# A 4096-cubed matmul with bias and tanh: the start reordered, with the first eight k-tiles in two blocks of four

One core of one Trainium2 chip. The metric is device time in microseconds (us) of one execution; the median of several runs is quoted.

## The reference

```python
def reference(a, b, bias):          # all float32, 4096 x 4096, bias 4096
    return np.tanh(np.matmul(a, b) + bias)
```

The kernel works in fp16: loads cast fp32 to fp16 on the way, issued from GpSimd.

## The kernel before

The matmul needs A with k on the partitions, so A must be turned. Column chunk 0 (1024 columns, two PSUM banks wide) is special: its start has nothing loaded yet, so row blocks 0 to 3 ("group 0", eight PSUM banks) go over k-tiles 0 to 7 first, then row blocks 4 to 7 ("group 1") over the same k-tiles, then both over k-tiles 8 to 15, and so on; partial sums are put aside in SBUF. I call each of the first passes of 64 matmuls a block of 64.

```python
KS = 8          # the k order of the first 8 k-tiles: k = 8*x + t, x = partition
def load_b_low(queue, dst, n0, t0, nt):           # B: every 8th row is one k-tile
    src = b[ds(0, P * KS), ds(n0, NCW)].rearrange("(x t) n -> x t n", t=KS)
    queue.dma_start(out=dst, in_=src[:, ds(t0, nt), :])
...
def load_nat(m):                                  # row-wise A, 4 KB runs, 8 k-tiles
    nc.gpsimd.dma_start(out=nat[m], in_=a[ds(m * P, P), ds(0, P * KS)]...)
def turn_nat(m):                                  # 8 TensorE transposes, 2 copies
    ...
# order of the queue: A0 A1 B1 A2 B2 A3 B3 B4 B5 B6 B7, then
want_a("g1a", 2, 4 * P, 2 * Q, 0, KS)             # row blocks 4,5: 4 loads of 128 KB
want_a("g1b", 2, 6 * P, 2 * Q, 0, KS)             # row blocks 6,7: 4 loads of 128 KB
want_a(("g0", KS), G, 0, G * Q, KS, KM - KS)      # group 0, k-tiles 8..15
... B k-tiles 8..15, group 1 k-tiles 8..15, A and B k-tiles 16..31, bias ...
for m in range(G):
    turn1(m, ("g1a", "g1b"), 0, KS)               # VectorE transposes
down(ps, KS - 2, KS, put_aside)                   # k-tiles 6,7 of group 0
group1(0, KS, put_aside, before1)                 # second block of 64
```

`load_a` issues one DMA for each quarter of 32 partitions and each stretch of k order, so for row blocks 8 to 31 and all later chunks 4 loads for k-tiles 0 to 7 and 4 for 8 to 31.

## Time and profile before

| | kernel before |
|---|---|
| median (3 runs; a fourth came with the result) | 1785.42 us (1785.22 to 1785.9) |
| profiled span | 1783.5 us |
| TensorE busy | 1776.8 us |
| second block of 64 starts | 25.25 us |
| third block starts | 39.08 us |
| sixth pass (row blocks 4 to 7, k-tiles 16 to 31) starts | 94.33 us |
| the remaining 7712 matmuls start | 121.96 us |

From 121.96 us on the kernel is one unbroken run of matmuls. The lines are in the prediction.

### The profile page before, as it was taken

Reading aid. Unit: us, or ns where it says so; the run is one execution under the profiler, and the core shown is the slowest. Engines: PE = TensorE matmul, PEld = TensorE weight load, DVE = VectorE, ACT = ScalarE, POOL = GpSimd, SP = SyncE. Lnnn points to the kernel's source line nnn. Section 1 sums busy time; section 2 is a strip of 40 time slices with the busy share of each in tenths; the row PEclk is TensorE's granted clock in tenths of the full one; section 3 lists DMA queues with packets and bytes.
Section 4 is the critical chain, followed back from the end, with each engine's and each line's share of the span. In section 5 each row is a group of like instructions: output and inputs, shape, how many; then the busy total and the mean of one; then the engine's idle time right before and its main releaser. Section 6 shows DMA issues by size and latency. Waiting matters only on the chain.

```text
span 1783.5 us, 20275 instructions
## 1 busy us (share of the span) xinstructions
PE 1776.8 (100%) x8272; PEld 808.7 (45%) x8272; DVE 856.6 (48%) x561; ACT 174.9 (10%) x281; POOL 607.3 (34%) x1126
## 2 busy tenths in 40 slices
PE   9999999999999999999999999999999999999999
PEld 4444444444444444444444444444444444444444
DVE  3774544455444544454444544454445544454442
ACT  3020000000000000000000000000000000000001
POOL 5454433232443333223343333223322233223310
PEclk9999999999999999999999999999999999999999
DMA  9999987676988866666698876666767666766731
GB/s 194 189 211 222 172 151 129 111 136 110 191 155 154 149 107 119 116 119 118 111 201 154 158 135 118 113 121 107 130 111 125 107 111 118 118 114 108 119 75 42
DMA packets 207916, 238.61 MB, mean 134 GB/s; under 512 B 22096, under 2 KB 157776, under 8 KB 207824
## 3 DMA queue, kind: packets, MB, share of 16 engines
q0 software_dynamic: 170384, 169.68, 65.2%
q1 hardware_dynamic: 37152, 67.52, 10.4%
q8 instruction: 64, 1.05, 0.2%
q14 instruction: 28, 0.23, 0.0%
q10 hardware_dynamic: 288, 0.13, 0.0%
HBM read 337.64 MB, written 67.11 MB: 227 GB/s over the span
## 4 chain that ended last, share of the span: by engine, by line
PE 99%; DMA 0%; issue 0%; POOL 0%; ACT 0%; DVE 0%; POOLq 0%; DVEq 0%
PE ps L404 93%; PE ps L134 6%; DMA nat<-in_a_dram 0%; POOL nat L231 0%; PE tp L243 0%; ACT o_sb L148 0%; DVE at L245 0%; DVE o_sb L145 0%; ACT at L246 0%; POOL b L68 0%; POOL ident L251 0%; POOLq L251 0%; DVEq L145 0%; POOLq L427 0%
## 5 line engine op out<-in xcount | busy, mean ns | idle before, releaser
L404 PE MATMUL ps<-b,at 128*128 128x512 f16 x7712 | 1657.8, 378 | 0.0
L404 PEld LDWEIGHTS <-at 128*128 128x128 f16 x7712 | 754.6, 98 | 903.3
L85 POOL DMA_DIRECT2D an<-in_a_dram x1004 | 542.4, 549 | 1059.4 <-DVE at L96 921.8
L96 DVE STREAM_TRANSPOSE at<-an 128x1024 f16<-128x1024 f16 x252 | 647.7, 2612 | 0.1
L145 DVE TENSOR_TENSOR o_sb<-ps,bias_bc 128x512 f32<-128x512 f32 (+1 forms) x243 | 166.2, 685 | 873.6 <-PE ps L404 752.4
L148 ACT ACTIVATE o_sb<-o_sb 128x512 f32<-128x512 f32 (+1 forms) x243 | 151.7, 625 | 1500.9 <-DVE o_sb L145 1500.9
L134 PE MATMUL ps<-b,at 128*128 128x512 f16 x256 | 56.4, 379 | 1.4 <-DVE at L245 1.0
L72 POOL DMA_DIRECT2D b<-in_b_dram x96 | 52.2, 548 | 14.3 <-DMA an<-in_a_dram 10.3
L134 PE MATMUL ps<-b,atx 128*128 128x512 f16 x256 | 55.8, 379 | 0.0
L134 PEld LDWEIGHTS <-at 128*128 128x128 f16 x256 | 24.8, 98 | 31.5 <-DVE at L245 1.9
L134 PEld LDWEIGHTS <-atx 128*128 128x128 f16 x256 | 24.9, 98 | 30.3 <-DVE atx L96 0.3
L96 DVE STREAM_TRANSPOSE atx<-an 128x1024 f16<-128x1024 f16 (+1 forms) x12 | 21.9, 1897 | 16.6 <-DMA an<-in_a_dram 16.6
L148 ACT ACTIVATE spill<-spill 128x512 f32<-128x512 f32 x16 | 9.9, 630 | 78.5 <-DVE spill L145 78.5
L68 POOL DMA_DIRECT2D b<-in_b_dram x13 | 8.3, 643 | 24.7 <-PE ps L404 22.6
L145 DVE TENSOR_TENSOR spill<-ps,spill 128x512 f32<-128x512 f32 x16 | 10.3, 675 | 9.0 <-PE ps L134 9.0
L176 DVE TENSOR_TENSOR spill<-spill,bias_bc 128x512 f32<-128x512 f32 x16 | 9.7, 683 | 7.3 <-DMA bias_bc<-in_bias_dram 7.3
L171 DVE TENSOR_TENSOR spill<-ps,spill 128x512 f32<-128x512 f32 x16 | 10.2, 676 | 4.3 <-PE ps L134 4.3
L168 ACT COPY spill<-ps 128x512 f32<-128x512 f32 x16 | 8.7, 605 | 15.7 <-PE ps L134 15.7
L245 DVE COPY at<-tp 128x512 f16<-128x512 f16 x4 | 1.7, 425 | 11.8 <-PE tp L243 11.8
L219 PE MATMUL ps<-zeros 128*128 128x512 f16 x16 | 5.5, 522 | 1.3 <-DVE zeros L215 1.3
L219 PEld LDWEIGHTS <-zeros 128*128 128x128 f16 x16 | 2.0, 128 | 4.3 <-issue 2.5
L243 PE MATMUL tp<-ident,nat 128*128 128x128 f16 x32 | 2.7, 228 | 0.4 <-DMA nat<-in_a_dram 0.3
(13 smaller groups left out, 12.9 us busy)
## 6 DMA issues: line engine op xcount, KB each, us to landing
an<-in_a_dram POOLq DMA_DIRECT2D x480, 192.0 KB, 6.5
out_dram<-o_sb SPq DMA_DIRECT2D x239, 256.0 KB, 3.4
an<-in_a_dram POOLq DMA_DIRECT2D x480, 64.0 KB, 2.5
b<-in_b_dram POOLq DMA_DIRECT2D x103, 256.0 KB, 8.5
b<-in_b_dram POOLq DMA_DIRECT2D x6, 1024.0 KB, 13.6
an<-in_a_dram POOLq DMA_DIRECT2D x32, 128.0 KB, 6.5
out_dram<-spill SPq DMA_DIRECT2D x16, 256.0 KB, 5.7
an<-in_a_dram POOLq DMA_DIRECT2D x12, 256.0 KB, 7.2
```

What stands on the lines that cost most here:

```text
L68: queue.dma_start(out=dst, in_=src[:, ds(t0, nt), :])
L72: nc.gpsimd.dma_start(out=bt[t0 // TB][ds(q * QP, QP), ds(t0 % TB, nt), :], in_=src.rearrange("(t p) n -> p t n", p=QP),)
L85: nc.gpsimd.dma_start(out=an[ds(q * QP, QP), :, ds((t - t0) * QP, n * QP)], in_=src.rearrange("(mb p) k -> p mb k", p=QP),)
L96: nc.vector.transpose(at[:, ds(t, n), :].rearrange("P t (mb p) -> P mb t p", p=QP), an[:, ds(mb0, Q), ds((t - t0) * QP, n * QP)].rearrange ...
L134: nc.tensor.matmul(ps, at[:, t, :], bt[t // TB][:, t % TB, ts(j, NB)], start=start, stop=stop)
L145: nc.vector.tensor_tensor(out=o_sb[:, piece], in0=ps[:, piece], in1=addend[:, piece], op=mybir.AluOpType.add)
L148: nc.scalar.activation(o_sb[:, piece], o_sb[:, piece], mybir.ActivationFunctionType.Tanh)
L168: nc.scalar.copy(aside(m, j), ps)
L171: nc.vector.tensor_tensor(out=aside(m, j), in0=ps, in1=aside(m, j), op=mybir.AluOpType.add)
L176: nc.vector.tensor_tensor(out=aside(m, j), in0=aside(m, j), in1=bias_bc[:, ts(j, NB)], op=mybir.AluOpType.add)
L219: nc.tensor.matmul(warm, zeros[:, :P], zeros, start=i == 0, stop=i == WARM - 1)
L404: nc.tensor.matmul(ps, at[:, t, :], b_cur[t // TB][:, t % TB, ds(c0, w)], start=t == 0, stop=t == KT - 1,)
```

## The change

The intent: start TensorE sooner. Cut the k order of the first eight k-tiles into two blocks of four. Then row-wise A needs only 128 KB (written) per row block for the first four k-tiles, and all four can go ahead of B's second tile. The second block of group 0 comes later, for VectorE; row block 4 is loaded row-wise and turned by TensorE in the middle of the pass. The core of the diff:

```diff
+    BL = 4
-    WARM = 16
+    WARM = 12
-        src = b[ds(0, P * KS), ds(n0, NCW)].rearrange("(x t) n -> x t n", t=KS)
+        src = b[ds(t0 // BL * BL * P, P * BL), ds(n0, NCW)].rearrange("(x t) n -> x t n", t=BL)
+    def split(t0, nt):           # load_a and transpose_a: 4 + 4 + rest, was 8 + rest
+        low = [(t, BL) for t in range(t0, min(t0 + nt, KS), BL)]
+        t = max(t0, KS)
+        return low + ([(t, t0 + nt - t)] if t0 + nt > t else [])
-    load_nat(0)
-    load_nat(1)
-    ... B1, A2, B2, A3, B3 .. B7
-    want_a("g1a", 2, 4 * P, 2 * Q, 0, KS)
-    want_a("g1b", 2, 6 * P, 2 * Q, 0, KS)
+    for m in range(G):
+        load_nat(m, 1)                       # A0 A1 A2 A3, k-tiles 0..3
+    for i in range(3):
+        want(load_b_next)                    # B1 B2 B3
+    want_a("g0a", 2, 0, 2 * Q, BL, BL)       # group 0, k-tiles 4..7: 8 loads of 64 KB
+    want_a("g0b", 2, 2 * P, 2 * Q, BL, BL)
+    for i in range(3):
+        want(load_b_next)                    # B4 B5 B6
+    want(lambda: load_nat(G, KS // BL))      # row block 4
+    want(load_b_next)                        # B7
+    want_a("g1a", 2, 5 * P, 2 * Q, 0, KS)    # row blocks 5,6: 8 loads of 64 KB
+    want_a("g1b", 1, 7 * P, Q, 0, KS)        # row block 7: 8 loads of 32 KB
... (loops of the first pass rewritten to match; row block 4 turned inside down())
```

More of the change, by code (lines that the diff above doesn't have):

```diff
@@ L65, in load_b_low @@
     def load_b_low(queue, dst, n0, t0, nt):
-        src = b[ds(0, P * KS), ds(n0, NCW)].rearrange("(x t) n -> x t n", t=KS)
-        queue.dma_start(out=dst, in_=src[:, ds(t0, nt), :])
+        src = b[ds(t0 // BL * BL * P, P * BL), ds(n0, NCW)].rearrange("(x t) n -> x t n", t=BL)
+        queue.dma_start(out=dst, in_=src[:, ds(t0 % BL, nt), :])
     def load_b(bt, n0, t0, nt, q):
@@ L75, in load_b @@
         )
+    def split(t0, nt):
+        low = [(t, BL) for t in range(t0, min(t0 + nt, KS), BL)]
+        t = max(t0, KS)
+        return low + ([(t, t0 + nt - t)] if t0 + nt > t else [])
     def load_a(m0, nmb, t0, nt):
         an = anat.tile([P, nmb, nt * QP], fp16, name="an")
-        parts = [(0, KS), (KS, t0 + nt - KS)] if t0 < KS < t0 + nt else [(t0, nt)]
-        for t, n in parts:
+        for t, n in split(t0, nt):
             for q in (0, 2, 1, 3):
-                k = q * KS * QP if t < KS else P * KS + (q * (KT - KS) + t - KS) * QP
+                k = t * P + q * BL * QP if t < KS else P * KS + (q * (KT - KS) + t - KS) * QP
                 src = a[ds(m0, nmb * QP), ds(k, n * QP)]
@@ L91, in transpose_a @@
     def transpose_a(at, an, mb0, t0, nt):
-        parts = [(0, KS), (KS, t0 + nt - KS)] if t0 < KS < t0 + nt else [(t0, nt)]
-        for t, n in parts:
+        for t, n in split(t0, nt):
             order = "P mb (k t) -> P mb t k" if t < KS else "P mb (t k) -> P mb t k"
@@ L194, in across, with down @@
                     mm(ps[m][j], ats[m], b_cur, t, j, t == first, False)
-    def down(ps, t0, t1, done):
+    def down(ps, t0, t1, done, before=None):
         for m in range(G):
+            if before:
+                before(m)
             for j in range(J):
@@ L225, with load_nat @@
     nc.scalar.copy(b_cur[0][:, 0, :], raw_b[:, 0, :])
-    nat = [opool.tile([P, P, KS], fp16, name=f"nat_{m}", tag="o_sb") for m in range(G)]
-    def load_nat(m):
+    def load_nat(m, blocks):
+        nat = opool.tile([P, blocks, P, BL], fp16, name="nat", tag="o_sb")
+        src = a[ds(m * P, P), ds(0, blocks * P * BL)]
         nc.gpsimd.dma_start(
-            out=nat[m], in_=a[ds(m * P, P), ds(0, P * KS)].rearrange("m (x t) -> m x t", t=KS)
+            out=nat, in_=src.rearrange("m (u x t) -> m u x t", u=blocks, t=BL)
         )
+        nats[m] = nat
     def load_b_next():
@@ L238, in load_b_next, with turn_nat @@
         load_b_low(nc.gpsimd, b_cur[t // TB][:, ds(t % TB, 1), :], 0, t, 1)
-    def turn_nat(m):
-        tp = psum.tile([P, KS, P], fp16, name="tp", tag="ps")
-        for t in range(KS):
-            nc.tensor.transpose(tp[:, t, :], nat[m][:, :, t], ident)
-        h = KS // 2
-        nc.vector.tensor_copy(ats[m][:, ds(0, h), :], tp[:, ds(0, h), :])
-        nc.scalar.copy(ats[m][:, ds(h, h), :], tp[:, ds(h, h), :])
-    b_done = [1]
-    load_nat(0)
-    load_nat(1)
+    def turn_nat(m, blocks, copy):
+        tp = psum.tile([P, blocks * BL, P], fp16, name="tp", tag="ps")
+        for t in range(blocks * BL):
+            nc.tensor.transpose(tp[:, t, :], nats[m][:, t // BL, :, t % BL], ident)
+        copy(ats[m][:, ds(0, blocks * BL), :], tp)
+    nats, b_done = {}, [1]
+    for m in range(G):
+        load_nat(m, 1)
     nc.gpsimd.affine_select(
@@ L254, with row @@
     )
-    load_b_next()
-    for m in (2, 3):
-        load_nat(m)
-        load_b_next()
-    while b_done[0] < KS:
-        load_b_next()
-    want_a("g1a", 2, 4 * P, 2 * Q, 0, KS)
-    want_a("g1b", 2, 6 * P, 2 * Q, 0, KS)
+    for i in range(3):
[4 more added lines that the diff above has]
+        want(load_b_next)
+    pump()
+    ps = []
+    def row(m, t0, nt):
+        if len(ps) == m:
+            ps.append([psum.tile([P, NB], fp32, name="ps") for j in range(J)])
+        across(ps, (m,), t0, nt, 0)
+    turn_nat(0, 1, nc.vector.tensor_copy)
+    turn_nat(1, 1, nc.scalar.copy)
+    row(0, 0, 1)
+    turn_nat(2, 1, nc.vector.tensor_copy)
+    row(1, 0, 1)
+    turn_nat(3, 1, nc.scalar.copy)
+    row(2, 0, 1)
+    row(3, 0, 1)
+    across(ps, range(G), 1, BL - 1, 0)
+    want(lambda: load_nat(G, KS // BL))
+    want(load_b_next)
+    want_a("g1a", 2, 5 * P, 2 * Q, 0, KS)
+    want_a("g1b", 1, 7 * P, Q, 0, KS)
     want_a(("g0", KS), G, 0, G * Q, KS, KM - KS)
@@ L277, with before0 @@
     todo = [(c, mi) for c in range(NC) for mi in range(MT) if (c, mi) >= (0, 2 * G)]
-    ps = []
-    def row(m, t0, nt):
-        if len(ps) == m:
-            ps.append([psum.tile([P, NB], fp32, name="ps") for j in range(J)])
-        across(ps, (m,), t0, nt, 0)
-    turn_nat(0)
-    turn_nat(1)
-    row(0, 0, 1)
-    row(1, 0, 1)
-    across(ps, (0, 1), 1, 1, 0)
-    turn_nat(2)
-    row(2, 0, 2)
-    across(ps, (0, 1, 2), 2, 1, 0)
-    turn_nat(3)
-    row(3, 0, 3)
-    across(ps, range(G), 3, KS - 2 - 3, 0)
-    def turn1(m, keys, t, nt):
-        turn(ats[G + m], keys[m // 2], (m % 2) * Q, t, nt)
+    for m in range(G):
+        turn(ats[m], "g0a" if m < 2 else "g0b", m % 2 * Q, BL, BL)
+    across(ps, range(G), BL, KS - 2 - BL, 0)
+    def before0(m):
+        if m == 2:
+            turn_nat(G, KS // BL, nc.vector.tensor_copy)
+    down(ps, KS - 2, KS, put_aside, before0)
     def turn0(m, t, nt):
         turn(ats[m], ("g0", t), m * Q, t, nt)
-    for m in range(G):
-        turn1(m, ("g1a", "g1b"), 0, KS)
-    down(ps, KS - 2, KS, put_aside)
     def before1(m, j):
         if m == G and j == 0:
+            turn(ats[5], "g1a", 0, 0, KS)
+            turn(ats[6], "g1a", Q, 0, KS)
+            turn(ats[7], "g1b", 0, 0, KS)
             for i in range(G):
@@ L318 @@
     for m in range(G):
-        turn1(m, ("g1c", "g1d"), KS, KM - KS)
+        turn(ats[G + m], "g1c" if m < 2 else "g1d", m % 2 * Q, KS, KM - KS)
     across(ps, range(G), KS, KM - 2 - KS, KS)
```

## The prediction

> **What bounds the kernel now.** I first read the busy rows of the page and the chain that ended last, then its start in order of time.
>
> ```profile
> span 1783.5 us, 20275 instructions
> PE 1776.8 (100%) x8272; PEld 808.7 (45%) x8272; DVE 856.6 (48%) x561; ACT 174.9 (10%) x281; POOL 607.3 (34%) x1126
> ```
>
> TensorE is busy over the whole span. The work is 32 k-tiles x 32 row blocks x 8 column banks = 8192 matmuls of 512 columns. The chain shows how little else there is:
>
> ```profile
> 8.07 2.15 PE L134 MATMUL ps<-b,at 128*128 128x512 f16 x8
> ...
> 11.58 2.33 PE L134 MATMUL ps<-b,at 128*128 128x512 f16 x10 [0.52 <-DVE at L245]
> ...
> 14.93 0.39 PE L134 MATMUL ps<-b,at 128*128 128x512 f16 x1 [0.52 <-DVE at L245]
> 15.54 9.87 PE L134 MATMUL ps<-b,at 128*128 128x512 f16 x45 [0.22 <-ACT at L246]
> 25.25 13.99 PE L134 MATMUL ps<-b,atx 128*128 128x512 f16 x64
> 39.08 13.98 PE L134 MATMUL ps<-b,at 128*128 128x512 f16 x64
> ```
>
> These are TensorE's lines in order of time (start, length, what). From 15.54 us to the end there is no gap. A block of 64 matmuls takes 39.08 - 25.25 = 13.83 us, 0.216 us each (the 379 ns that the page gives as the mean of one is a latency). So only two things can move the time: when the gapless run begins, counted by how many matmuls were done before it, and whether the change opens a new gap later. I use one marker: the start of the second block of 64 (row blocks 4 to 7 on k-tiles 0 to 7), 25.25 us now. Whatever moves it moves the end.
>
> Before 15.54 us 19 matmuls are done (4.1 us of work), so 11.4 us of the span are lost there. After 8.07 us the loss is 25.25 - 8.07 - 64 x 0.216 = 3.4 us, mostly the 16 late transposes of A and waits for their copies. The idle that the change attacks is thus at most about 5 us: 1.5 us of earlier first matmul and 3.4 us, against 1785.
>
> What feeds that start? The transfers:
>
> ```profile
> nat<-in_a_dram POOLq DMA_DIRECT2D x4, 256.0 KB, 6.2
> ```
>
> ```profile
> DMA packets 918, 1.66 MB, mean 207 GB/s; under 512 B 101, under 2 KB 110, under 8 KB 918
> ```
>
> ```profile
> DMA packets 3159, 1.55 MB, mean 194 GB/s; under 512 B 132, under 2 KB 3159, under 8 KB 3159
> ```
>
> The second fence is the DMA view from 10 to 18 us (2 KB packets), the third from 20.5 to 28.5 us (512 B packets). Both windows are full, at about 200 GB/s of written fp16. In the records the 256 KB loads land every 1.25 us (12.77, 14.03, 15.31, 16.52, 17.78, 19.09 us), so the start is a saturated queue. B's last low tile (k-tile 7, eleventh in the queue) lands at 19.09 us:
>
> ```profile
> L68 POOL DMA_DIRECT2D b<-in_b_dram x1: 531/531/531, 9.0 to 9.0; - x1
> ...
> DMA to landing us min/median/max: 10.1/10.1/10.1
> ```
>
> TensorE wants it only at 25.25 - 16 x 0.216 = 21.8 us: 2.7 us of slack. That slack is what the change can spend.
>
> **What the Trainium skill says.** "DMA: Bandwidth & Descriptors", section "Why small descriptors are slow (HBM only)", gives each packet a fixed overhead of a few cycles; its "Specifications" want at least 512 B for line rate. The trace agrees mildly down to 512 B: from 2048 to 512 B the rate drops from 207 to 194 GB/s. It has no 256 B load, which is what the change makes. "TensorE: Matmul & The Clock Gate", section "Part 1: The HAM clock gate", says about 3.4 us of work warm the array and that an idle window as long cools it. In the trace the warm-up matmuls go from 0.43 us apart to 0.215 at 5.08 us, 3.8 us after the first. Twelve of them end at about 5.5 us, so cutting 16 to 12 is safe, provided that no wait comes near 3.4 us.
>
> **The change part by part.**
>
> *Earlier first matmul.* Row-wise A loads halve (128 KB written each) and all four go ahead of B's tile 1. They take the queue places that two old ones had: half-sized steps on the old landings (5.88, 7.48, 8.73, 10.30) put them at about 5.3, 5.9, 6.7 and 7.5 us. Four transposes each (8 took 0.71 us), a copy of 0.42 us on VectorE or 0.59 on ScalarE: first matmul at about 6.6 us instead of 8.07, k-tile 0 finished at about 9.2. B tiles 1 to 3 are queue places 3 to 5 and land at about 8.75, 10.3 and 11.55, so TensorE runs without a gap to about 14.4 us with 32 matmuls done, where the old kernel had 19 at 15.54.
>
> *Then the queue is the bound.* Before B's tile 7, the old queue held 4 x 256 of A plus 7 x 256 KB of B: 2816 KB. The new one holds 512 KB of row-wise A, 512 KB of A's second block (8 loads of 64 KB in 256 B packets), 256 KB of row block 4 and 1792 KB of B: 3072 KB, 256 KB more, hence 1.25 us. Packets: from 1.25 us for sixteen 2048 B packets per engine and 0.67 us for sixteen of 512 B, one packet costs about 4 ns + 0.0746 ns/B; 256 B then take 23 ns, 176 GB/s, 0.38 us per 64 KB (estimate, a straight line beyond its points). Eight of them cost 3.0 instead of 2.5 us, and the 1 KB packets another 0.1 us. B's tile 7 then lands at 19.09 + 1.25 + 0.5 + 0.1 = 21.0 us. The same arithmetic puts B's tile 4 at 15.9 us: TensorE waits 14.4 to 16.0 there, and again about 1.6 us for tile 7, because at 19.4 us it has done everything else. Behind tile 7 lie 16 matmuls (3.45 us) and the 8 transposes of row block 4 (about 0.8): the second block of 64 begins at about 21.1 + 4.3 = 25.4 us. That is **0.15 us later** than now. The 256 KB more ahead of tile 7 eat the slack, so the better beginning buys nothing.
>
> *What comes after.* A's load for row blocks 5 to 7 is now 16 loads, in 64 and 32 KB pieces. GpSimd needs 0.55 to 0.58 us to issue each, more than the 0.2 us that a 32 KB piece moves for; also an issue waits until the load eight before it has landed (the issue at 9.02 us follows the landing at 8.73). I put A and B for k-tile 8 about 3 us later than now, B's at 39 to 40 us against 35.96. TensorE wants it at 39.2, so a stall of 0 to 0.8 us is possible there: I add **0.2 us**. Transposes for row blocks 5 to 7 must be ready from about 28.9 us on, with data about 25 us and 2.1 us of VectorE for a block:
>
> ```profile
> L96 DVE STREAM_TRANSPOSE atx<-an 128x1024 f16<-128x1024 f16 x4 | 8.0, 2170 | 8.1 <-DMA an<-in_a_dram 8.1
> ```
>
> They are in time.
>
> *The other 1700 us.* The order view shows that each later row block now has 12 loads of A instead of 8 (120 row blocks, 480 more issues) and three VectorE transposes instead of two. GpSimd: 14 issues with B's two x 0.55 = 7.7 us in the 13.8 us of a row block. DMA: 512 packets of 512 B become 1024 of 256 B, 16 x (2 x 23 - 41) = 80 ns per 64 KB on an engine, 0.16 us a row block. VectorE: one fixed cost of some 0.1 us. TensorE is fed two row blocks ahead, so all of it lies beside the matmuls: **0**.
>
> *Sum.* 0.15 + 0.2 = 0.35 us; the uncertainty of 256 B packets is one-sided (150 GB/s instead of 176 adds about 0.5 us on tile 7's landing, 100 GB/s adds 2.2), so I put the centre at +0.6: 1785.42 + 0.6 = **1786.0 us**.
>
> **Rivals.**
> 1. *The whole early gain survives.* If tile 7 did not bind, the second block would begin at 6.6 + 64 x 0.216 + 2 = about 22.4 us: 1782.6. For it: TensorE's idle at 10 to 15 us does go away. Against it: the queue is full from 5 us on at 207 GB/s, and 3072 KB cannot be through by 18 us. A quicker queue start by half a us would give 1785.
> 2. *256 B packets are slow* (100 GB/s or less). Then A's second block takes 5.2 us, tile 7 lands at 23.2, the second block starts at 27.6, and k-tile 8 comes late too: 1788 to 1789. For it: the page's 512 B rule. Against: the small loss from 2048 to 512 B.
> 3. *Steady state opens gaps.* Were the later row blocks bound by DMA or by GpSimd's issues, each 0.1 us a row block would cost 12 us. Against it: VectorE's transposes have 0.1 us of idle before them in 252 instances, so they never wait for loads now, and the sums above stay below 13.8 us. I give it 2%.
>
> **Range and chances.** Between a queue half a us quicker and rival 2 nearly in full: 1784.7 to 1788.0 us. Two per cent are 36 us; faster by that is impossible (8192 matmuls at 0.2154 us, the mean over the chain from 15.54 to 1776.3 us, are 1765 us of the 1783.5), slower needs rival 3 at full size.
>
> **What would show it.** Right: the first 512-column matmul with B near 6.6 us, two TensorE gaps of 1 to 2 us near 14.4 and 19.4 us with DMA of B as the releaser, the block on row block 4 starting near 25.4 us, none or one short gap near 39 us, then none. Wrong: tile 7 landing before 20 us (faster) or after 22 (slower), or any gap past 60 us.

## The result, and the profile after

The changed kernel took 1789.55 us (median of 4, 1789.04 to 1790.22), beside 1785.55 for the kernel before (4 runs): **4.0 us slower**, ratio 1.0023, 95% interval 1.0005 to 1.004. A ratio is the mean time of one kernel's runs over that of the other's of the same rounds, so not quite the ratio of the medians. The prediction was +0.6 us with a range up to 1788.0: wrong.

TensorE's lines in order of time, as in the prediction's first table (start, length, what, and in brackets the idle time before and what ended it):

```profile
9.48 6.04 PE L138 MATMUL ps<-b,at 128*128 128x512 f16 x26 [0.21 <-ACT at L252]
17.53 3.83 PE L138 MATMUL ps<-b,at 128*128 128x512 f16 x17 [2.01 <-DMA b<-in_b_dram]
22.96 1.67 PE L138 MATMUL ps<-b,at 128*128 128x512 f16 x7 [1.61 <-DMA b<-in_b_dram]
...
26.64 13.98 PE L138 MATMUL ps<-b,atx 128*128 128x512 f16 x64
42.45 13.97 PE L138 MATMUL ps<-b,at 128*128 128x512 f16 x64 [1.83 <-DMA b<-in_b_dram]
...
98.45 27.79 PE L138 MATMUL ps<-b,atx 128*128 128x512 f16 x128 [0.59 <-DVE spill L149]
126.08 1657.84 PE L418 MATMUL ps<-b,at 128*128 128x512 f16 x7712
```

There are two waits for B's tiles 4 and 7, then one for k-tile 8, then one for VectorE. The last row has the same 1657.84 us as before, to the digit: the steady state costs nothing. All of the loss is in the start of the long run, 126.08 - 121.96 = 4.12 us. Counted by stage, after against before:

| stage | before | after | adds |
|---|---|---|---|
| second block starts | 25.25 | 26.64 | +1.39 |
| from there to the third block | 13.83 | 15.81 | +1.98 |
| sixth pass, from the start of the fifth | 27.63 | 28.37 | +0.74 |
| sum | | | +4.11 |

The fifth pass starts at 66.70 before and at 70.08 after, which with 94.33 and 98.45 gives the third row. In the records of the loads, B's tile 7 lands at 22.92 us instead of 19.09, the last part of B's k-tile 8 at 42.32 instead of 35.96, the bias at 85.79 instead of 79.42. So the transfers are 3.8 us late at tile 7 and 6.4 us late at k-tile 8. Why so much more at k-tile 8? Busy time by engine in stretches of 5 us (the last two columns are the DMA engines' busy share and GB/s written); first before, then after:

```profile
25.00:30.00 5.00, 5.00 (x24) 2.17 (x23) 5.00 (x4) 2.62 (x5) 2.49 (x6) 1.00 1.40 200
```

```profile
25.00:30.00 5.00, 5.00 (x26) 2.27 (x24) 3.88 (x7) 3.07 (x6) 5.00 (x9) 1.00 0.72 62
30.00:35.00 5.00, 5.00 (x25) 2.25 (x23) 0.51 (x1) 1.76 (x3) 3.93 (x8) 1.00 1.34 175
```

The fifth engine column is GpSimd (POOL): it is busy for all 5.00 us with 9 issues, and the DMA engines move 62 GB/s where they had moved 200. The queue ran dry while GpSimd issued loads of 32 KB one after the other, 0.53 us apart. VectorE (third column) isn't the brake: it was busier, 5.00 us, in the kernel before. The DMA view of the same kernel from 25.5 to 29.5 us shows what was issued (KB are bytes written; the fp32 read is twice as long):

```profile
DMA packets 1060, 0.24 MB, mean 60 GB/s; under 512 B 1060, under 2 KB 1060, under 8 KB 1060
...
an<-in_a_dram POOLq DMA_DIRECT2D x5, 32.0 KB, 2.4
```

And from 11.8 to 14.8 us of the same kernel, with 64 KB loads queued up and the engines full until 14 us (GB/s in 40 slices):

```profile
GB/s 150 208 140 195 164 188 164 157 181 178 167 188 161 174 178 167 191 161 171 184 164 181 164 167 191 164 174 171 133 120 89 65 62 62 68 65 65 113 116 154
```

The first 28 slices are near 175 GB/s although nearly every packet has 256 B. The dip at the end, before B's tile 4, is again a queue that ran dry.

The chain that ended last says it from the other side. Its middle pieces (start, length, what):

```profile
23.85 3.50 POOL an L90 x7
27.35 0.25 issue
27.60 2.45 POOL an L90 x4
30.05 7.26 DMA an<-in_a_dram
37.31 0.28 issue
37.60 9.73 DMA b<-in_b_dram
...
74.98 10.81 DMA bias_bc<-in_bias_dram
85.88 2.57 DVE spill L180 x5
```

Before, this chain left the loads at 10.3 us, went through transposes and copies, and was matmul alone from 15.5 us on:

```profile
3.44 6.87 DMA nat<-in_a_dram
...
15.54 106.58 PE ps L134 x493
```

Now it goes through eleven issues on GpSimd (23.85 to 30.05; by the records eight of 32 KB loads and three of the 256 KB loads behind them), then through loads that each wait for the one eight places ahead, to the bias, to VectorE's additions of the bias, to the sixth pass. The wait for the load eight places ahead is the program's own: in the trace GpSimd's loads use eight semaphores in turn (99 to 106), and an issue waits on the one that it uses itself (recorded for 1466 of 1618; e.g. the issue at 10.42 us behind a landing at 10.13). More semaphores, for a deeper backlog, no run tried.

The hole at 62 GB/s is not the whole delay. The last 32 KB load lands at 29.68, 4.1 us later than the last load for row blocks 4 to 7 did before (25.61), which is hardly more than the 3.8 of tile 7, but 256 KB less had to be moved. Two of the four 256 KB loads behind it then land 2.41 and 2.50 us after the load ahead of them, where it had been 1.29 and 1.33: another 2.3 us. What slows these two no run shows by itself; where the small loads are merged (e2) the first takes 1.76 and the other 1.36.

My theory after reading this (A): the stages are gates in series. A gate is a point at which TensorE can't go on before something has landed. Each is opened by a load; the last late gate sets the end, an earlier one only matters where the next doesn't close behind it. What closes them is above all the number of issues. The rival (B): tile 7's lateness is the cause and goes through to the end. A third: the 256 B packets are slow in themselves.

### The profile page after: what moved, and what is told of

The parts are those of the page before. It is cut to its first block, busy times and chain, and to the rows that moved or that the text cites. A ratio compares the mean times of both kernels' runs of the same rounds, so it can differ in the third digit from the quotient of the medians.

```text
span 1787.6 us, 20882 instructions
## 1 busy us (share of the span) xinstructions
PE 1776.0 (99%) x8260; PEld 807.7 (45%) x8260; DVE 766.5 (43%) x686; ACT 173.4 (10%) x279; POOL 873.8 (49%) x1623
## 4 chain that ended last, share of the span: by engine, by line
PE 94%; DMA 4%; POOL 1%; issue 1%; DVE 1%; ACT 0%; DVEq 0%; POOLq 0%
PE ps L418 93%; DMA b<-in_b_dram 3%; PE ps L138 2%; DMA an<-in_a_dram 1%; DMA bias_bc<-in_bias_dram 1%; DVE spill L180 0%; POOL an L90 0%; POOL nat L238 0%; POOL b L69 0%; ACT o_sb L152 0%; DVE atx L100 0%; DVE spill L149 0%; DVE o_sb L149 0%; POOL ident L257 0%; POOLq L257 0%
## 5 line engine op out<-in xcount | busy, mean ns | idle before, releaser
L90 POOL DMA_DIRECT2D an<-in_a_dram x1500 | 808.8, 547 | 804.4 <-DVE at L100 560.3
L100 DVE STREAM_TRANSPOSE at<-an 128x3072 f16<-128x3072 f16 (+2 forms) x376 | 563.3, 1548 | 128.6 <-DMA an<-in_a_dram 128.5
L100 DVE STREAM_TRANSPOSE atx<-an 128x512 f16<-128x512 f16 (+2 forms) x14 | 17.7, 1298 | 9.4 <-DMA an<-in_a_dram 9.4
L172 ACT COPY spill<-ps 128x512 f32<-128x512 f32 x16 | 8.8, 593 | 23.0 <-PE ps L138 22.9
```

The source lines that it names most:

```text
L90: nc.gpsimd.dma_start(out=an[ds(q * QP, QP), :, ds((t - t0) * QP, n * QP)], in_=src.rearrange("(mb p) k -> p mb k", p=QP),)
L100: nc.vector.transpose(at[:, ds(t, n), :].rearrange("P t (mb p) -> P mb t p", p=QP), an[:, ds(mb0, Q), ds((t - t0) * QP, n * QP)].rearrange ...
L172: nc.scalar.copy(aside(m, j), ps)
```

## The experiments

Unless stated, an edit is to the changed kernel. "Over before" is the difference of the medians of the same rounds, on the same chip (the kernel before took 1785.5 to 1786.7 in the four sets of rounds). Times of stages are from one trace of each kernel, and the kernel before has one, of a run of 1785.48. In the rounds of e1 to e4 and e9 to e12 its median was 1.0 to 1.2 us above that run, so that a difference of medians is there about as much more favourable to the edits than the stages show.

**e1: tile 7 ahead of row block 4.**

```diff
-    want(lambda: load_nat(G, KS // BL))
     want(load_b_next)
+    want(lambda: load_nat(G, KS // BL))
```

> B's tile 7 queued ahead of row block 4, so 256 KB leave the path to tile 7. Theory A (the stages are gates in series and the last late one sets the end; k-tile 8 of B and then the bias come too late because the transfers as a whole run late): the second block of 64 starts about 1.1 us earlier (25.5 instead of 26.64 us), but the stall for k-tile 8 grows by as much, the third block still starts at 42.4 and the time stays at 1789.5 (+-0.4). Theory B (the end is set by the late tile 7, each us gained there is a us at the end): 1788.4.

Measured: 1790.26 us, 3.6 over before, ratio 1.0019. The second block starts at 26.07 us, 0.6 sooner than in the changed kernel, the third not before 43.00. What was gained was lost again at once, as theory A says; the time is above its 1789.5 (+-0.4). There was more: TensorE's weight loads after that wait.

```profile
43.00 15.66 PE L138 MATMUL ps<-b,at 128*128 128x512 f16 x64 [2.95 <-DMA b<-in_b_dram]
43.75 0.15 PEld L138 LDWEIGHTS <-at 128*128 128x128 f16 x1 [0.22 <-issue]
44.18 0.15 PEld L138 LDWEIGHTS <-at 128*128 128x128 f16 x1 [0.28 <-issue]
44.60 0.15 PEld L138 LDWEIGHTS <-at 128*128 128x128 f16 x1 [0.28 <-issue]
```

They come 0.43 us apart until 47.06, as at the very start: a wait of 2.95 us cost half speed for over 3 us, 1.7 us more. So in this run one longer wait was dearer than two short ones. Tile 7 itself gained 0.57 us, not 1.1, since B's tile 5 landed 0.9 us late in this run.

**e2: row blocks 5 to 7 in one set of loads**, 8 of 96 KB for 8 of 64 and 8 of 32 KB; bytes and packets the same.

```diff
-    want_a("g1a", 2, 5 * P, 2 * Q, 0, KS)
-    want_a("g1b", 1, 7 * P, Q, 0, KS)
+    want_a("g1a", 3, 5 * P, 3 * Q, 0, KS)
```

> Row blocks 5 to 7 loaded by 8 loads of 96 KB instead of 8 of 64 and 8 of 32 KB: same bytes, same 256 B packets, half the issues. Theory A with the cause in the issues (GpSimd issues one load per 0.55 us, 32 KB move in 0.2, so the queue ran dry at 62 GB/s from 25 to 30 us): the hole goes, tile 8's B lands at about 38 instead of 42.3 us, no stall at the third block, bias 4 us earlier, no gap at 98 us; second block unchanged at 26.6; time 1786.8. Rival (the 256 B packets themselves are slow): queue as slow as before, 1789.5. Theory B: no change, 1789.5.

Measured: 1786.79 us, 0.1 over before, ratio 1.0001 (0.9986 to 1.0016). The stretch from 25 to 30 us, and TensorE from the second block on:

```profile
25.00:30.00 5.00, 5.00 (x28) 2.31 (x26) 3.37 (x6) 3.23 (x7) 4.05 (x8) 1.00 1.55 181
```

```profile
26.80 13.98 PE L138 MATMUL ps<-b,atx 128*128 128x512 f16 x64
40.62 13.98 PE L138 MATMUL ps<-b,at 128*128 128x512 f16 x64
54.43 13.98 PE L138 MATMUL ps<-b,atx 128*128 128x512 f16 x64
```

62 GB/s became 181 with the same 256 B packets; k-tile 8 lands at 38.60 instead of 42.32; no wait follows the second block, and the sixth pass has none either. The two last gates, 2.7 of the 4.1 us, came from the number of issues. The second block is as late as before the edit (26.80), and by the stages that remains at the end: the long run starts at 123.50 us, 1.54 later than in the kernel before, so the 0.1 us of the medians flatter the edit. Theory B and the theory of slow packets fall.

**e3: the bias load ahead of the loads for k-tiles 16 to 31.**

```diff
     SA = [(KM, 8), (KM + 8, 8)]
+    want(lambda: load_bias(bias_bc, 0, nc.gpsimd))
     ...
-    want(lambda: load_bias(bias_bc, 0, nc.gpsimd))
```

> The bias load moved ahead of the A and B loads for k-tiles 16 to 31. Theory A: only the last gate goes (the 0.6 to 0.7 us gap at 98 us, where VectorE adds the bias late); second and third block start as in the changed kernel (26.6 and 42.4 us); time 1788.8. Theory that the late bias load sets the end alone whatever else: back to 1785.5.

Measured: 1788.92 us, 2.3 over before, ratio 1.0011. Second and third block start at 27.29 and 43.07 us; the gap ahead of the sixth pass is gone (98.32 - 70.69 = 27.63, the value of the kernel before). The gate is confirmed in the trace; it is worth 0.74 there. The ratio (0.9994 to 1.0028) doesn't settle it alone. The time moved by more than that, with runs of one kernel spread over 1.2 us, so I take the size from the stages.

**e4: all of it**: e1, e2 and e3, and A's second block of group 0 as 4 loads of 128 KB.

```diff
-    want_a("g0a", 2, 0, 2 * Q, BL, BL)
-    want_a("g0b", 2, 2 * P, 2 * Q, BL, BL)
+    want_a("g0a", G, 0, G * Q, BL, BL)
```

> All of it: tile 7 first, row blocks 5 to 7 in one set of loads, A's second block of row blocks 0 to 3 as 4 loads of 128 KB instead of 8 of 64, bias early. Theory A: tile 4 lands about 0.6 us earlier, tile 7 at about 20.7, second block at about 25.0 us, no later gap: 1785.2. Theory B: 1787.9 or so (only tile 7's gain). If late B tile 1 (landing at 10.1 us) recurs, it costs up to 1 us of this.

Measured: 1784.15 us, **2.5 under before**, ratio 0.9986 (0.9971 to 1.0001).

```profile
16.62 5.49 PE L138 MATMUL ps<-b,at 128*128 128x512 f16 x24 [1.38 <-DMA b<-in_b_dram]
...
24.13 13.98 PE L138 MATMUL ps<-b,atx 128*128 128x512 f16 x64
37.94 13.98 PE L138 MATMUL ps<-b,at 128*128 128x512 f16 x64
```

One wait for B is left, and the long run starts at 120.82 us, 1.14 before that of the kernel before; this is the size by the stages, and most of the rest of the 2.5 us is the slower median of the kernel before in these rounds. Tile 7 lands at 20.32. The intent of the change works with larger loads, with tile 7 and the bias moved ahead; how much of it the larger loads do alone is for e12.

e5, e6 and e8 look for what made the first B tile late: in every profile with four A loads in a row it lands 1.8 to 2.5 us behind the last of them (2.41 in the changed kernel), where a load of that size mostly takes 1.25.

**e5: the all-in version (e4) with B's tile 1 after the second A load.**

> The all-in version with B's tile 1 moved between the second and the third row-wise load of A. In all five profiles with blocks of four, B's tile 1 landed 2.0 to 2.5 us after the load ahead of it, a load of that size else takes 1.25. Theory C (the first B tile on this queue is slow wherever it stands): it lands some 2.2 us after the second A load, everything after it as in the all-in version (tile 7 at 20.3, second block at 24.1), time 1784.2. Theory D (four A loads ahead of it in a row, or their issues, make it slow): it lands 1.3 us after the second A load, tile 7 at 19.3, second block at 23.1, time 1783.1.

Measured: tile 1 lands 1.29 us behind the second A load (6.54 to 7.83), as theory D has it; in the repeat (e11) it was 1.66 (6.50 to 8.16), between D and C. But tile 7 lands at 19.81, between D's 19.3 and C's 20.3, the second block starts at 23.77, and the time is 1784.09 us, 1.6 under before (0.9992). D holds for tile 1 in this run; only half of the gain reached tile 7.

**e6: B's rows at the old spacing (wrong result)**, on the all-in version: `"(x t) n -> x t n"` with t=8 over the first 1024 rows for B's low tiles of chunk 0.

> WRONG RESULT ON PURPOSE: the all-in version, but B's low tiles of the first column chunk are read from every eighth row as in the kernel before, not from every fourth. Theory S (reading every fourth row makes B's tiles land late): tile 1 lands 1.3 us after the last A load, at about 9.2, tile 7 at 19.3, second block at 23.1. Otherwise tile 1 about 2 us after it, 24.1. Result incorrect either way.

Measured, one run of unknown state: result incorrect as intended (relative error 0.47), 1783.41 us. Tile 1 landed 1.98 us behind the last A load (7.19 to 9.17), in e4 it was 1.95. The spacing of B's rows isn't it. The expectation named 9.2 us as the sign of the spacing, and tile 1 did land there, but because A's fourth load landed 0.7 us sooner in this run; the distance is what counts.

**e7: the kernel before, with its eight 128 KB loads of A for row blocks 4 to 7 split into 32 of 32 KB**, packets of 512 B as ever.

```diff
+    h = nmb // pieces                # pieces = 4 for g1a and g1b, else 1
+    for i in range(pieces):
+        src = a[ds(m0 + i * h * QP, h * QP), ds(k, n * QP)]
+        nc.gpsimd.dma_start(out=an[ds(q * QP, QP), ds(i * h, h), ...], in_=...)
```

> The kernel BEFORE with one thing changed: the eight 128 KB loads of A for row blocks 4 to 7 become 32 loads of 32 KB, with the same 512 B packets. Theory A (issues on GpSimd bind, 0.55 us each, whatever the packets): 32 x 0.55 = 17.6 us instead of 5.4 of transfer, queue at 60 GB/s or so, B for k-tile 8 lands at about 46 instead of 36 us, time about 1793 (+7 to +9). Rival (only 256 B packets hurt, loads of 32 KB don't): 1786.5, as the kernel before of the same rounds.

Measured: 1796.53 us, 10.9 over before, ratio 1.006 (1.0043 to 1.0077). The DMA view from 22 to 33 us:

```profile
DMA packets 1679, 0.69 MB, mean 63 GB/s; under 512 B 336, under 2 KB 1679, under 8 KB 1679
...
an<-in_a_dram POOLq DMA_DIRECT2D x22, 32.0 KB, 2.2
```

63 GB/s, the same as in the changed kernel, with 512 B packets and without any other part of the change: it is the issues. VectorE isn't it here either: from 30 to 35 us it is busy for 1.16 us, and 62 GB/s are moved. 22 issues in 11 us are 0.5 us each, and 32 KB in 0.53 us are 62 GB/s. The time exceeded my +7 to +9. The second block had waits of 1.49 and 1.36 us for row blocks turned late. Then TensorE waited 4.97 us for k-tile 8 and took 15.09 us for a block that takes 13.83, at half speed again at first:

```profile
47.94 15.26 PE L136 MATMUL ps<-b,at 128*128 128x512 f16 x64 [4.97 <-DMA b<-in_b_dram]
63.03 13.98 PE L136 MATMUL ps<-b,atx 128*128 128x512 f16 x64
```

**e8: the all-in version with A's second block of group 0 behind B's tile 7.**

> The all-in version with A's second block of row blocks 0 to 3 queued behind B's tiles 4 to 7 instead of ahead of tile 4. It is a probe of tile 1: if the issues of many-row loads next to it slow it, it lands 1.3 us after the last A load; if not, 2 us or more, as ever. TensorE must wait for A's second block until about 20.5 us and then do 32 matmuls, so the second block of 64 comes 4 us or more later than in the all-in version (28 to 30), with a half-speed stretch after that wait if it is long enough to cool the array: in the run with tile 7 first, a wait of 3.0 us at 40 us was followed by matmuls 0.43 us apart for 3.7 us. Time 1788 to 1790.

Measured, one run of unknown state: 1790.73 us, second block at 30.79, both just beyond what was expected. Tile 1 lands 2.23 us behind the last A load (7.60 to 9.83): issues of small loads beside it don't seem to be the cause either, though one of the four was still issued then (7.88 us). TensorE's wait of 5.97 us was followed by half speed; the column after GpSimd's is the granted clock:

```profile
20.00:25.00 5.00, 3.82 (x10) 1.30 (x11) 2.49 (x4) 0.00 (x0) 4.18 (x7) 0.50 1.71 177
```

**e9: the changed kernel again.**

> The changed kernel itself once more, beside the versions below: +3.5 to +4.5 us on the kernel before of the same rounds, ratio 1.0022. In its profile the same three late starts again: second block 26.5 to 27.3 us, a stall of 1.5 to 2.5 us before the third block, up to 0.8 us before the last block of row blocks 4 to 7.

Measured: 1790.57 us, 4.1 over before, ratio 1.0021 (1.0008 to 1.0033). Second block at 27.21 us, a wait of 1.69 us before the third, 0.73 before the sixth pass: the three gates are no accident of one trace.

```profile
18.14 5.08 PE L138 MATMUL ps<-b,at 128*128 128x512 f16 x15 [2.50 <-DMA b<-in_b_dram]
...
42.88 13.97 PE L138 MATMUL ps<-b,at 128*128 128x512 f16 x64 [1.69 <-DMA b<-in_b_dram]
...
99.02 27.79 PE L138 MATMUL ps<-b,atx 128*128 128x512 f16 x128 [0.73 <-DVE spill L149]
```

In this profile the wait for tile 4 was 2.50 us and was followed by half speed from 19.5 to 22.9 us; in the first profile the wait of 2.01 us was not.

**e10: the all-in version again.**

> The all-in version again: 1.5 to 2.5 us below the kernel before, ratio 0.9988; second block near 24.1 us, no later stall.

Measured: 1784.31 us, 2.1 under before, ratio 0.9987 (0.9975 to 1.0); second block at 24.58.

**e11: the version of e5 again.**

> The all-in version with B's tile 1 sooner, again: 0 to 0.7 us below the all-in version in the same rounds; second block 23.5 to 24.1.

Measured: 1784.00 us, 2.4 under before, ratio 0.9986 (0.9972 to 0.9999), 0.3 under e10 in the same rounds; second block at 24.23, tile 7 at 20.39 (20.76 in e10, 20.32 in e4). Every run of e4, e10 and e11 (1783.76 to 1784.61) is below every run of the kernel before (1785.22 and more), so they beat it, by 0.7 to 1.1 us in the stages and 2.1 to 2.5 in the medians; e11 against e10 isn't clear.

**e12: only the two merges of loads.**

> The changed kernel with both sets of small loads merged (A's second block of row blocks 0 to 3: 4 loads of 128 KB instead of 8 of 64; row blocks 5 to 7: 8 of 96 KB instead of 16), nothing else. If the lateness of B's tile 4 (1.83 us behind the small loads instead of 1.25) came from its issue waiting for a small load eight places ahead: tile 4 1.2 to 1.3 us behind the last small load, second block at about 26.0 us (26.8 with row blocks 5 to 7 merged alone), no later stall; 0.3 to 1 us above the kernel before. Of the 2.7 us that the all-in version gained on the second block that leaves about 1.3 to tile 7's place in the queue.

Measured: 1785.60 us, 0.8 under before, ratio 0.9995 (0.9983 to 1.0008); second block at 25.20, no wait after it. That is better than the 26.0, and 0.3 to 1 us above the kernel before, that were expected; by the stages the long run starts at 121.90, level with the kernel before. Part of it is that tile 3 landed 0.45 us sooner in this run than in the changed kernel's first profile. Tile 4 lands 1.31 us behind the last small load (15.17 to 16.48), in the changed kernel 1.83. From tile 3 to tile 7 it took 9.25 us (12.23 to 21.48), in the changed kernel 10.24, in e10 with tile 7 first 7.69. The prediction's own sum for this stretch is 3.0 (small loads) + 4 x 1.25 (tiles 4 to 7) + 1.3 (row block 4) = 9.3: right in the run where no issue was late.

## Why the prediction was wrong, step by step

In sum: 0.35 us were forecast by stages and 4.1 came. Of the 3.8 us between, 1.2 are the second block's, 1.8 the third's, 0.7 the sixth pass's. Two of the prediction's own signs of being wrong came true: tile 7 landed after 22 us, and there was a gap past 60 us.

- *What bounds the kernel, and the marker* (start of the second block): the bound was right. But "whatever moves it moves the end" was not: the prediction used one marker where there were three gates in a row, and in e1 the marker came sooner and the end no sooner.
- *Earlier first matmul* at 6.6 us: measured 7.32. The twelve warm-up matmuls were all at half speed and held TensorE until 6.36 us, while the first A load was there at 5.10. Harmless: the queue bound what followed.
- *Queue as the bound, 256 KB more ahead of tile 7*: the mechanism was right, with two waits for tiles 4 and 7, from 15.5 and 21.4 us (announced near 14.4 and 19.4). Its size was off: tile 7 at 22.92 instead of 21.0. Of these 1.9 us, 1.1 were there at tile 3 already (12.68 against 11.55; the first B tile was slow), 0.5 came ahead of tile 4, 0.3 behind it. Ahead of tile 4 the last small load could be issued only at 12.96 us, when tile 3, eight places ahead of it, had landed (12.68); tile 4's issue stood behind it, and the queue ran dry. Where A's second block is four loads (e12) tile 4 isn't late. So the second block came 1.39 us later, not 0.15.
- *256 B packets at 176 GB/s* by a straight line through 512 and 2048 B: right. The small loads landed every 0.37 us for 64 KB (13.06 to 15.66 us for the last seven steps), where 0.38 was predicted. (Two slips in the working change no sum: 256 KB in packets of 2048 B are eight, not sixteen, packets on each of 16 engines, and the line was fitted to eight; the 80 ns of the steady state are for 128 KB, not 64.) Yet I widened the range for this term and not for the next.
- *What comes after*: this is the step that failed. The prediction saw that GpSimd needs 0.55 us to issue a load whose data take 0.2, and then put k-tile 8 "about 3 us later than now, B's at 39 to 40 us", a stall of 0.2 us. It came 6.4 us later, at 42.32, a stall of 1.98. Of the 3.4 us beyond the forecast 1.9 were there at tile 7 already; the rest arose behind it. e2 and e7 show the cause: the number of issues, those of 32 KB coming in a row at some 60 GB/s, and in e2 tile 7 is as late (23.08) and yet no stall follows. The prediction doesn't show how it came to 3 us; the backlog of earlier transfers couldn't hide these issues, because at most eight loads are under way at once: the 64 KB loads ahead had landed by 25.97 us, and the last 32 KB load was issued at 27.60.
- *"none or one short gap near 39 us, then none"*: wrong. The bias is at the end of the same queue, 6.4 us late, and the 16 additions of the bias on VectorE then hold up the sixth pass by 0.74 us. e3 removes it. The prediction had not looked at what waits behind the loads of k-tiles 16 to 31.
- *Steady state costs 0*: right, 1657.84 us in both kernels, with 480 more issues on GpSimd (497 more in all) and a third transpose a row block.
- *Rivals*: number 2 came nearest to the measured 1789.55, with 1788 to 1789, for a reason that the runs refute (e2 kept the packets and lost the stalls).

What stays open: why the first B tile is slow behind four A loads, 1.1 of the 1.9 us at tile 7. The spacing of B's rows (e6) isn't it, and small-load issues beside it (e8) hardly are, by one run each; moving it ahead of two A loads helped tile 1 and only half of it reached tile 7 (e5). In the packet records single packets that start near 7 us take up to 1.9 us in the changed kernel where 0.17 is usual, and none as much as 1.1 us in the kernel before; what delays them no run here shows. Open too is what slows the two 256 KB loads behind the small ones.

## What to carry to other kernels

When a change splits loads, count the issues as a resource of their own: size of a load over the issue time is a bandwidth, and here 32 KB over 0.53 us is 62 GB/s, against 175 to 200 for the same packets in larger loads. Follow a late transfer through the queue to every later consumer, down to the smallest load at its end; a start-up is a row of gates, and a gain at one of them counts only if the next is open. Keep waits of TensorE short: here those of 2.5 us and more were followed by some microseconds at half speed, those of 2.0 us and less were not.

## What the Trainium skill lacked or had wrong

- "DMA: Bandwidth & Descriptors", section "Issuing engines are not separate DMA queues", calls the time to initiate a DMA "usually small relative to the DMA itself". For loads of 32 KB it is the larger of the two: 0.53 to 0.55 us an issue on GpSimd, some 0.2 us of transfer, 60 to 63 GB/s (changed kernel and e7). Its "Rules for kernel authors" do say that under 64 KB one pays mostly overhead; the page gives no time for a whole issue from GpSimd.
- The same page, section "Specifications", asks for at least 512 B for line rate. Loads that cast fp32 to fp16, with packets of 256 B as written (512 B as read), ran at about 175 GB/s, against 194 at 512 B and 207 at 2048 B as written: a mild loss.
- "TensorE: Matmul & The Clock Gate", section "Part 1: The HAM clock gate", puts cooling at an idle window of about 3.4 us or more. Waits of 2.95 us (e1) and 2.50 us (e9) were followed by half speed (3.33 and 2.88 us from the start of the matmul before to that of the one after); waits of 1.4 to 2.0 us were not.
